# Mixer A of a hybrid decoder: contiguous copies of the normed operands in the dilated order, and attention heads taken two at a time

## The chip, the cores and the metric

The kernel runs on one core of a Trainium2 chip. Five engines work side by side in it: TensorE (PE in the profile; its weight loads are listed as PEld), VectorE (DVE), ScalarE (ACT), GpSimd (POOL) and SyncE (SP), which issues most of the DMAs. The metric is the device time of one execution in microseconds (us), smaller is better. Times are the median of several runs; rows come from one profiled execution.

## The reference, cut to what matters

A trunk of two layers over 512 tokens of width 1024, all in float32. Each layer is half a SwiGLU, a block of three token mixers A, B and C on the same normed `u`, and another half SwiGLU. The change touches mixer A, dilated attention with 3 groups x 6 heads of 64 columns:

```python
DIL_PAIRS = ((128, 1), (512, 4), (2048, 16))     # (window, dilation), 6 heads each
u = rms_norm(h, g_mix)
proj = u @ w_in
a = proj[..., :A_IN].reshape(B, S, 3, A_GROUPS, A_SLOTS, HEAD_DIM)
qa, ka = apply_rope(a[:, :, 0], cos, sin), apply_rope(a[:, :, 1], cos, sin)
o_a = dilated_attention(qa, ka, a[:, :, 2])
...
# dilated_attention: for each group, keys gathered by stride `dil`
    o, lse = banded_attention(to_sub(q), to_sub(k), to_sub(v), BLOCK_Q, n_prev, steps)
alpha = softmax(stack(lses), axis=0)             # the groups of a head are combined
o = sum(alpha[..., None] * stack(outs), axis=0)
```

Group 0 (dilation 1) works on the tokens in their order, groups 1 and 2 on the tokens `c, c+4, c+8, ...` for c = 0 to 3.

## The kernel before, in words

**Products in three parts.** Every large product is made of three float32r matmuls: each operand is split into a high part and the rest, and high x high, low x high and high x low are added up in PSUM. The normed activations lie as eight pairs of tiles `gh[k]`, `gl[k]` (128 features x 512 tokens), the weights are split as they arrive (`whi` on ACT in line 358, `wlo` on DVE in line 359).

**Input projections.** `project_in` multiplies with the activations as the stationary operand: for 8 blocks k of features and 4 blocks j of 128 tokens it issues three matmuls (line 649 ff.), with the 128 tokens of block j as weights of the array and 384 (or 512, 280) columns of `w_in` moving. With `dil` true, block j is every fourth token: the stationary operand is read from `gh` and `gl` with a step of 4 elements. That is so for the groups g = 1 and 2 of mixer A and for nothing else: 3 head pairs p x 2 groups x 8 k x 4 j x 2 layers = 384 such triples of matmuls, all with 384 moving columns.

**Mixer A's attention.** A unit `a_unit(l, p)` does two heads (h = 0 and 1, rows 0 to 63 and 64 to 127 of the tiles `qa`) over all three groups; there are 6 units. All its matmuls are in plain float32, which the trace shows as two records of a weight load and a matmul each. First the scores: for each head, each kind of group (`grp` 1: groups 1 and 2 together; 0: group 0) and each pair `ip` of query blocks, one PSUM bank `sps` is filled by matmuls that contract over the head's 64 rows; DVE adds the mask and takes the minimum (line 1336), ACT makes the exponentials (line 1338) into a tile `ea`. Then four small matmuls with `selT`, a chain of small DVE operations, four with `sel` (`ay`), and on POOL the scaling of the `ea` tiles (line 1370). Last, for each head and block, up to four transposes of `ea` into a bank `tps`, a copy `pa` (DVE or ACT), and up to four matmuls `pv` that write the head's 64 rows of the bank `ops`; the weights there are 64 columns of V, and 128 columns of `pa` move.

**Order of the work.** PE's instructions run in the order in which the program writes them. `weave` merges two things into that order: the stream of projections (`proj`, `project_in`) and the units of attention, which are generators that give up their turn with an estimated delay (`yield "", 1200`); the delay is counted on a clock that `mm` advances with each matmul. The other engines' instructions are ordered by a scheduler. Units wait for flags (`self.done`), so that much of a unit of mixer A for p = 0 or 1 has other projections between its pieces, but its last part has little: the next projection waits for the unit's end.

**Buffers.** PSUM has 4 banks `acc` (projections), 1 `sps`, 2 `tps`, 1 `ops`. The pool of the mixers (`mp`) is opened in `begin_mix`, at the first projection of mixer C.

Of the kernel before, what the change touches and what calls it, by code (L numbers as in the profile page):

```python
# [17 lines left out]
KD = D // 128  # L18
# [37 lines left out]
class Trunk:  # L56
# [567 lines left out]
    def project_in(self, l, cols, kn, dil, evac, pre=None, post=None, ready=None, after=()):  # L624
# [7 lines left out]
        def entries():  # L632
            for ci, k0 in enumerate(range(0, KD, kn)):
                srcs, o = [], 0
                for c, w in cols:
                    srcs.append((o, w, W[k0 * 128:(k0 + kn) * 128, c:c + w]))
                    o += w

                def use(hi, lo, k0=k0, ci=ci):
                    if k0 == 0:  # L640
                        if pre:
                            pre()
                        ps.extend(self.acc() for _ in range(4))
# [159 lines left out]
    def c_inputs(self, l, p):  # L803
# [338 lines left out]
    def b_cmp_probs(self, l, g):  # L1142
        nc = self.nc

        def make(U):
# [18 lines left out]
            small = lambda n: mp.tile([128, 4, 4], F32, tag=n, name=n, bufs=2)  # L1164
# [137 lines left out]
    def a_unit(self, l, p):  # L1302
        nc = self.nc

        def make(U):
# [6 lines left out]
            for h in range(2):  # L1312
                rows = slice(64 * h, 64 * h + 64)
                for grp in (1, 0):
                    for ip in range(2):
                        ps = self.sps()
                        e = mp.tile([128, 512], F32, tag="nq", name="ea", bufs=4) if h else self.et("ea")
                        spans = []
                        for iq in range(2):
                            i = 2 * ip + iq  # L1320
                            c0 = iq * 256 + (128 if grp == 0 and i == 0 else 0)
                            n = iq * 256 + 256 - c0
                            qc = slice(i * 128, (i + 1) * 128)
                            if grp == 0:
                                self.mm(ps[:, c0:c0 + n], qk[0][0][rows, qc],
                                        qk[0][1][rows, (i + 1) * 128 - n:(i + 1) * 128], start=True, stop=True)
                            else:
                                for g in range(2):
                                    self.mm(ps[:, c0 + g * 128:c0 + (g + 1) * 128], qk[1 + g][0][rows, qc],
                                            qk[1 + g][1][rows, qc], start=True, stop=True)  # L1330
                            spans.append((i, slice(c0, c0 + n), n))
# [7 lines left out]
                        es[grp, h, ip] = e  # L1339
                        yield "", 1200  # L1340
# [54 lines left out]
            def pv(h, grp, ip, lo, pa):  # L1395
                rows = slice(64 * h, 64 * h + 64)
                for c in range(lo, 512, 128):
                    iq, b = divmod(c // 128, 2)
                    i = 2 * ip + iq
                    if grp == 0:  # L1400
                        self.mm(Ov[rows, i], vs[0][:, i - 1 + b, rows], pa[:, c:c + 128],
                                start=(ip == 0 and c == lo), stop=False, skip_group_check=True)
                    else:
                        self.mm(O[rows, i * 128:(i + 1) * 128], vs[1 + b][:, i, rows], pa[:, c:c + 128],
                                start=False, stop=(ip == 1 and c == 384), skip_group_check=True)

            for n, (h, grp, ip) in enumerate(todo):
                T = self.tps()
                lo = 128 if grp == 0 and ip == 0 else 0
                for c in range(lo, 512, 128):  # L1410
                    self.transpose(T[:, c:c + 128], es[grp, h, ip][:, c:c + 128])
                pa = mp.tile([128, 512], F32, tag=("ph", "pl")[n % 2], name="pa", bufs=1)
                if n % 2:
                    nc.vector.tensor_copy(pa[:, lo:], T[:, lo:])
                else:
                    nc.scalar.activation(pa[:, lo:], T[:, lo:], AF.Copy)
                if pas:
                    pv(*pas.pop())
                pas.append((h, grp, ip, lo, pa))
                yield "", 1300  # L1420
# [22 lines left out]
    def begin_mix(self, l):  # L1443
# [9 lines left out]
        for u in range(2):  # L1453
# [4 lines left out]
            self.pz.append((ph, pl))  # L1458

# [162 lines left out]
```

## Time and profile before

| what | value |
|---|---|
| time, median of 3 runs (lowest to highest) | 2948.06 us (2946.42 to 2949.58) |
| profiled execution: time | 2947.3 us |
| profiled execution: span of the records | 2945.6 us |
| mean granted TensorE clock, share of full speed | 0.997 |
| PE busy, share of the span | 99% |
| PEld busy | 85% |
| DVE, ACT, POOL busy | 50%, 40%, 17% |
| DMA, mean share of the 16 engines over the span | about 30% |

The profiled execution's own time is 1.7 us above its span and 0.8 us below the median. The busy share of PE counts matmuls that overlap one another, so it says that PE had always something under way, not how fast it went. How fast it goes is read from the distance of the starts of successive matmuls, called the step below.

### The profile page before, as it was taken

How to read it: one execution, taken by the hardware profiler on the slowest of the kernel's cores; microseconds unless marked ns; L12 is line 12 of the kernel's file. 1: busy time of each engine (PE TensorE's matmuls, PEld its weight loads, DVE VectorE, ACT ScalarE, POOL GpSimd, SP SyncE). 2: the span in 40 equal slices, each digit the busy share in tenths (PEclk: the TensorE clock that was granted, in tenths of full speed). 3: DMA queues.
4: the chain of work that ended last, by engine and by line, in shares of the span. 5: the costliest groups of instructions: out<-in, count | busy, mean ns of one | idle time of the engine just before them, and what ended most of it. 6: DMA issues, size and time to landing. Idle time of an engine off the chain costs nothing.

```text
span 2945.6 us, 38966 instructions
## 1 busy us (share of the span) xinstructions
PE 2910.4 (99%) x14281; PEld 2499.2 (85%) x14281; DVE 1459.1 (50%) x2861; ACT 1175.6 (40%) x2405; POOL 506.4 (17%) x657
## 2 busy tenths in 40 slices
PE   8999999999999999999999999999999999999998
PEld 7888898898899888888888888988988998888886
DVE  5464356556633455444354434565665334644433
ACT  4333255455533334333233333554554333333332
POOL 2120012223210322110011100122231112311100
PEclk9999999999999999999999999999999999999999
DMA  4333333321222243333333333332123122433332
GB/s 123 100 94 105 108 97 88 106 63 62 76 60 54 74 126 102 98 97 96 101 93 94 100 103 118 90 101 85 54 65 83 49 56 72 146 97 95 99 93 79
DMA packets 295119, 265.14 MB, mean 90 GB/s; under 512 B 14232, under 2 KB 278544, under 8 KB 294928
## 3 DMA queue, kind: packets, MB, share of 16 engines
q1 hardware_dynamic: 289152, 255.05, 29.7%
q10 hardware_dynamic: 5776, 7.60, 0.7%
q8 instruction: 112, 1.84, 0.3%
q14 instruction: 79, 0.65, 0.1%
HBM read 248.97 MB, written 13.63 MB: 89 GB/s over the span
## 4 chain that ended last, share of the span: by engine, by line
PE 95%; issue 2%; DVE 1%; POOL 1%; ACT 0%; DMA 0%; ACTq 0%; DVEq 0%; POOLq 0%
PE acc L82 66%; PE ops L82 9%; PE tps L82 8%; PE sps L82 8%; PE tps L102 4%; DVE wlo L359 0%; POOL e L853 0%; POOL ss L292 0%; ACT whi L358 0%; DMA gr<-in_cmp_pe_v_dram 0%; POOL e L850 0%; POOL f L850 0%; PE acc L102 0%; DVE x L1084 0%; DVE cf L1087 0%
## 5 line engine op out<-in xcount | busy, mean ns | idle before, releaser
L359 DVE TENSOR_TENSOR wlo<-raw,whi 128x512 fp32r<-128x512 f32 (+3 forms) x944 | 650.7, 694 | 937.1 <-ACT whi L358 887.6
L358 ACT ACTIVATE whi<-raw 128x512 fp32r<-128x512 f32 (+3 forms) x944 | 565.3, 602 | 1113.3 <-PE acc L82 819.6
L82 PE MATMUL acc<-gh,whi 128*128 128x512 f32 x1088 | 430.7, 396 | 0.0
L82 PE MATMUL acc<-gh,wlo 128*128 128x512 f32 x1088 | 424.5, 390 | 0.0
L82 PE MATMUL acc<-gl,whi 128*128 128x512 f32 x1088 | 424.3, 390 | 0.0
L82 PE MATMUL acc<-whi,gh 128*128 128x384 f32 (+2 forms) x960 | 365.7, 381 | 0.0
L82 PE MATMUL acc<-wlo,gh 128*128 128x384 f32 (+2 forms) x960 | 350.1, 365 | 0.0
L82 PE MATMUL acc<-whi,gl 128*128 128x384 f32 (+2 forms) x960 | 350.0, 365 | 0.0
L530 POOL TENSOR_TENSOR a<-a,Rb 128x512 f32<-128x512 f32 x88 | 130.2, 1503 | 907.2 <-DVE a L529 907.2
L82 PE MATMUL acc<-hh,whi 128*128 128x512 f32 x704 | 274.2, 390 | 0.0
L82 PE MATMUL acc<-hh,wlo 128*128 128x512 f32 x704 | 273.9, 389 | 0.0
L82 PE MATMUL acc<-hl,whi 128*128 128x512 f32 x704 | 273.9, 389 | 0.0
L82 PEld LDWEIGHTS acc<-whi,gh 128*128 128x128 f32 x960 | 233.5, 243 | 13.6 <-issue 6.3
L82 PEld LDWEIGHTS acc<-gh,wlo 128*128 128x128 f32 x1088 | 204.2, 188 | 43.8 <-DVE wlo L359 0.2
L82 PEld LDWEIGHTS acc<-wlo,gh 128*128 128x128 f32 x960 | 235.6, 245 | 5.2
L82 PEld LDWEIGHTS acc<-whi,gl 128*128 128x128 f32 x960 | 235.9, 246 | 4.6
L82 PEld LDWEIGHTS acc<-gh,whi 128*128 128x128 f32 x1088 | 204.6, 188 | 39.8 <-issue 1.0
L82 PEld LDWEIGHTS acc<-gl,whi 128*128 128x128 f32 x1088 | 204.6, 188 | 38.2
L82 PEld LDWEIGHTS acc<-hh,wlo 128*128 128x128 f32 x704 | 132.2, 188 | 27.5
L82 PEld LDWEIGHTS acc<-hh,whi 128*128 128x128 f32 x704 | 132.2, 188 | 27.2
L82 PEld LDWEIGHTS acc<-hl,whi 128*128 128x128 f32 x704 | 132.2, 188 | 27.2
L82 PE MATMUL tps<-gh,whi 128*128 128x512 f32 x320 | 124.5, 389 | 0.0
(354 smaller groups left out, 4599.9 us busy)
## 6 DMA issues: line engine op xcount, KB each, us to landing
raw<-in_ffn_w_dram SPq DMA_DIRECT2D x256, 512.0 KB, 3.7
raw<-in_w_in_dram SPq DMA_DIRECT2D x288, 128.0 KB, 2.4
raw<-in_w_gate_dram SPq DMA_DIRECT2D x48, 512.0 KB, 3.5
raw<-in_w_in_dram SPq DMA_DIRECT2D x16, 512.0 KB, 3.7
raw<-in_w_out_dram SPq DMA_DIRECT2D x16, 512.0 KB, 4.2
gate<-gt ACTq DMA_DIRECT2D x28, 256.0 KB, 2.2
gt<-gate SPq DMA_DIRECT2D x28, 256.0 KB, 3.1
raw<-in_w_up_dram SPq DMA_DIRECT2D x16, 384.0 KB, 3.2
```

The source lines that it names most:

```text
L82: self.nc.tensor.matmul(out, lhsT, rhs, start=start, stop=stop, **kw)
L102: self.nc.tensor.transpose(out, in_, self.ident[:n, :n])
L358: nc.scalar.activation(hi, x, AF.Copy)
L359: nc.vector.tensor_tensor(lo, x, hi.bitcast(F32), op=ALU.subtract)
L530: nc.gpsimd.tensor_tensor(v[j], v[j], self.Rb, op=ALU.mult)
```

## The change

Four edits:

1. A new function `dilate` copies the eight tiles `gh[k]` into eight new tiles `gd[k]` on POOL, in the order in which every fourth token stands together. It is called as the projection of mixer C for p = 1 begins. `project_in` takes its high part from `gd` where `dil` is true, as a contiguous block of 128 columns; the low part `gl` is still read with the step of 4.
2. In the scores of `a_unit` the loop over the heads is the innermost one: matmuls of head 0 (bank `sps`) and head 1 (bank `tps`) alternate, and a turn ends after both heads (an estimated delay of 2400 instead of 1200).
3. The last part does the same: transposes of both heads into the two banks `tps`, a copy of head 0 on ACT and of head 1 on DVE, then `pv` with the heads alternating; four turns with a delay of 2600 instead of eight of 1300. Two more tags hold the copies.
4. Room for the `gd` tiles: two small tiles of mixer B get one buffer instead of two, and a scratch area for DMA descriptors is made smaller.

```diff
@@ project_in
                             xh, xl = tok(self.gh[g], j), tok(self.gl[g], j)
+                            if dil:
+                                xh = self.gd[g][:, j * 128:(j + 1) * 128]
                             self.mm(p, xh, hi[k], start=(g == 0), stop=False)
                             self.mm(p, xl, hi[k], start=False, stop=False)
                             self.mm(p, xh, lo[k], start=False, stop=(g == KD - 1))
@@ c_inputs, pre
             if p == 0:
                 self.begin_mix(l)
+            elif p == 1:
+                self.dilate()
@@ a_unit, scores
-            for h in range(2):
-                rows = slice(64 * h, 64 * h + 64)
-                for grp in (1, 0):
-                    for ip in range(2):
-                        ps = self.sps()
...
+            for grp in (1, 0):
+                for ip in range(2):
+                    pss = (self.sps(), self.tps())
...
+                        for g in range(2) if grp else (None,):
+                            for h, ps in enumerate(pss):
+                                rows = slice(64 * h, 64 * h + 64)
+                                if grp == 0:
+                                    self.mm(ps[:, c0:c0 + n], qk[0][0][rows, qc],
+                                            qk[0][1][rows, (i + 1) * 128 - n:(i + 1) * 128], start=True, stop=True)
+                                else:
                                     self.mm(ps[:, c0 + g * 128:c0 + (g + 1) * 128], qk[1 + g][0][rows, qc],
                                             qk[1 + g][1][rows, qc], start=True, stop=True)
...
-                        yield "", 1200
+                    yield "", 2400
@@ a_unit, last part
-            todo = [(h, grp, ip) for h in range(2) for grp in range(2) for ip in range(2)]
+            todo = [(grp, ip) for grp in range(2) for ip in range(2)]
...
+                    for h in range(2):
+                        rows = slice(64 * h, 64 * h + 64)
+                        if grp == 0:
+                            self.mm(Ov[rows, i], vs[0][:, i - 1 + b, rows], pa[h][:, c:c + 128],
+                                    start=(ip == 0 and c == lo), stop=False, skip_group_check=True)
...
+                for h in range(2):
+                    T = self.tps()
+                    for c in range(lo, 512, 128):
+                        self.transpose(T[:, c:c + 128], es[grp, h, ip][:, c:c + 128])
...
+                yield "", 2600
@@ new function
+    def dilate(self):
+        self.gd = []
+        for k in range(KD):
+            t = self.mp.tile([128, 512], F32R, tag=f"gd{k}", name="gd")
+            self.nc.gpsimd.tensor_copy(t.rearrange("p (c m) -> p m c", c=4), self.gh[k].rearrange("p (m c) -> p m c", c=4))
+            self.gd.append(t)
```

On PE, the first scores of the first unit (p = 0 of layer 0), with the end of the dilated projection before them and its continuation behind. Before (`acc<-whi,gh` reads: bank `acc`, from the weights' high part moving and `gh` standing):

```order
L82 MATMUL acc<-whi,gh 128x384
L82 MATMUL acc<-whi,gl 128x384
L82 MATMUL acc<-wlo,gh 128x384
L82 MATMUL sps<-qa 128x128 x4
L82 MATMUL acc<-whi,gh 128x384
L82 MATMUL acc<-whi,gl 128x384
```

and now:

```order
L82 MATMUL acc<-whi,gd 128x384
L82 MATMUL acc<-whi,gl 128x384
L82 MATMUL acc<-wlo,gd 128x384
L82 MATMUL sps<-qa 128x128
L82 MATMUL tps<-qa 128x128
L82 MATMUL sps<-qa 128x128
L82 MATMUL tps<-qa 128x128
L82 MATMUL sps<-qa 128x128
L82 MATMUL tps<-qa 128x128
L82 MATMUL sps<-qa 128x128
L82 MATMUL tps<-qa 128x128
```

Two of the three stationary operands of a triple are `gd`; the block of scores has eight matmuls of two heads in turn where it had four of one head, and a unit has four such blocks instead of eight, with 15, 15, 15 and 21 projection matmuls behind them instead of 9 (seven times) and 15.

On PE, the last part of the same unit. Before:

```order
L102 MATMUL tps<-ident,ea 128x128 x4
L82 MATMUL ops<-pa,va 64x32x4 x3
L102 MATMUL tps<-ident,nata 128x128 x4
L102 MATMUL tps<-ident,ea 128x128 x4
L82 MATMUL ops<-pa,va 64x32x4 x4
L102 MATMUL tps<-ident,ea 128x128 x4
L82 MATMUL ops<-pa,va 64x128 x4
L102 MATMUL tps<-ident,nata 128x128 x4
```

and now:

```order
L102 MATMUL tps<-ident,ea 128x128 x8
L82 MATMUL ops<-pa,va 64x32x4 x6
L82 MATMUL acc<-whi,gd 128x384
L82 MATMUL acc<-whi,gl 128x384
L82 MATMUL acc<-wlo,gd 128x384
L102 MATMUL tps<-ident,nata 128x128 x4
L102 MATMUL tps<-ident,ea 128x128 x8
L82 MATMUL ops<-pa,va 64x32x4 x8
L102 MATMUL tps<-ident,nata 128x128 x4
L102 MATMUL tps<-ident,ea 128x128 x8
```

Transposes (`ident,ea`) and `pv` matmuls (`pa,va`) come in blocks twice as long and half as many. In the units for p = 0 and 1 there are 8 blocks of `pv` before and 4 now, in those for p = 2 there are 7 and 4.

On POOL, where the copies stand now in layer 0 (`a<-a,Rb`: the last multiplications of the first half SwiGLU; `f` and `e`: the first masks and products of mixer C):

```order
L530 TENSOR_TENSOR a<-a,Rb 128x512 x8
L1475 COPY gd<-gh 128x128x4 x8
L854 AFFINE_SELECT f<-f 128x128
L854 AFFINE_SELECT e<-e 128x128
L854 AFFINE_SELECT f<-f 128x128
L857 TENSOR_TENSOR e<-e,f 128x127
```

Before, the masks of mixer C came next to those multiplications; now the eight copies are ahead of them in POOL's queue, in both layers.

## Rows read from the trace of the kernel before

**Rows 1.** The profile's page: busy time, share and instructions of PE and PEld, and the shares of the span along the chain that ended last, by engine.

```profile
PE 2910.4 (99%) x14281; PEld 2499.2 (85%) x14281; DVE 1459.1 (50%) x2861; ACT 1175.6 (40%) x2405; POOL 506.4 (17%) x657
...
PE 95%; issue 2%; DVE 1%; POOL 1%; ACT 0%; DMA 0%; ACTq 0%; DVEq 0%; POOLq 0%
```

**Rows 2.** PE's instructions in order of time (start us, duration us, engine, line, op, out<-in, shapes). First an unbroken run of 30 matmuls of a dilated projection, its first and its last; then an unbroken run of 95 of a projection in token order (group 0), its first and its last.

```profile
816.74 0.40 PE L82 MATMUL acc<-whi,gh 128*128 128x384 f32 x1
...
823.51 0.40 PE L82 MATMUL acc<-wlo,gh 128*128 128x384 f32 x1
...
889.31 0.34 PE L82 MATMUL acc<-whi,gl 128*128 128x384 f32 x1
...
905.60 0.34 PE L82 MATMUL acc<-wlo,gh 128*128 128x384 f32 x1
```

**Rows 3.** Groups of weight loads (count | busy us, mean ns of one): in a stretch of the second run of rows 2, in a stretch of the first, and over the whole program.

```profile
L82 PEld LDWEIGHTS acc<-wlo,gh 128*128 128x128 f32 x31 | 5.8, 188 | 0.0
...
L82 PEld LDWEIGHTS acc<-wlo,gh 128*128 128x128 f32 x9 | 3.0, 330 | 0.0
...
L82 PEld LDWEIGHTS acc<-wlo,gh 128*128 128x128 f32 x960 | 235.6, 245 | 5.2
```

**Rows 4.** The place where a projection in token order ends (816.56 is its last matmul) and a dilated one begins: PE and then PEld in order of time. The load that starts at 816.57 is the first with a step, that of the matmul at 816.74.

```profile
816.56 0.34 PE L82 MATMUL acc<-wlo,gh 128*128 128x384 f32 x1
...
816.97 0.41 PE L82 MATMUL acc<-whi,gl 128*128 128x384 f32 x1
...
816.39 0.19 PEld L82 LDWEIGHTS acc<-wlo,gh 128*128 128x128 f32 x1
816.57 0.31 PEld L82 LDWEIGHTS acc<-whi,gh 128*128 128x128 f32 x1
816.78 0.33 PEld L82 LDWEIGHTS acc<-whi,gl 128*128 128x128 f32 x1
817.02 0.33 PEld L82 LDWEIGHTS acc<-wlo,gh 128*128 128x128 f32 x1
```

**Rows 5.** The chain of waits in the first unit of mixer A, in order of time (start us, length us, engine and bank, line, records): blocks of scores (`sps`, 8 records are 4 matmuls) and the projection between them, and the 21 projection matmuls between the small matmuls with `selT` and those with `sel`.

```profile
837.51 1.09 PE sps L82 x8
838.59 2.36 PE acc L82 x9
840.95 1.08 PE sps L82 x8
...
866.77 5.07 PE acc L82 x21
```

**Rows 6.** Groups over the whole program (records | busy us, mean ns of one): the matmuls of scores and of `pv`, the `selT` matmuls, the weight loads of both, and the copies `pa` out of a bank `tps` on DVE.

```profile
L82 PE MATMUL ops<-pa,va 128*64 128x128 f32 x360 | 49.2, 279 | 0.0
L82 PE MATMUL sps<-qa 64*128 64x128 f32 x216 | 33.5, 289 | 0.7 <-DVE asm L1336 0.7
L82 PE MATMUL sps<-qa 64*128 64x256 f32 x72 | 20.7, 394 | 0.0
...
L82 PE MATMUL tps<-asm,selT 128*128 128x16 f32 x48 | 5.8, 252 | 0.0
...
L82 PEld LDWEIGHTS ops<-pa,va 128*64 128x64 f32 x360 | 38.0, 136 | 7.7 <-issue 7.4 <-ACT whi L358 0.3
L82 PEld LDWEIGHTS sps<-qa 64*128 64x128 f32 x288 | 37.4, 187 | 12.8 <-issue 8.8 <-DVE wlo L359 1.4 <-PE acc L82 1.1
...
L1414 DVE COPY pa<-tps 128x512 f32<-128x512 f32 x24 | 16.5, 689 | 25.9 <-PE tps L102 25.9
```

**Rows 7.** Runs of like records on PE, merged, from the start of the first to the end of the last: inside a block of scores of 128 columns (six records), of scores of 256 columns (three), of the `selT` matmuls with 16 moving columns (seven), and of `pv` (six); then, whole, a block of `pv`, one of transposes and the next of `pv`.

```profile
837.76 0.83 PE L82 MATMUL sps<-qa 64*128 64x128 f32 x6
...
861.40 0.81 PE L82 MATMUL sps<-qa 64*128 64x256 f32 x3
...
865.84 0.93 PE L82 MATMUL tps<-asm,selT 128*128 128x16 f32 x7
...
886.67 0.82 PE L82 MATMUL ops<-pa,va 128*64 128x128 f32 x6
...
886.41 1.09 PE L82 MATMUL ops<-pa,va 128*64 128x128 f32 x8
887.42 0.66 PE L102 MATMUL tps<-ident,nata 128*128 128x128 f32 x4
888.01 1.09 PE L82 MATMUL ops<-pa,va 128*64 128x128 f32 x8
```

**Rows 8.** POOL ahead of mixer C in layer 0 (the bracket is its idle time before the row and what ended it), the last of the tiles `gh` on ACT, and POOL's group of 128x512 products.

```profile
414.59 0.29 POOL L850 TENSOR_SCALAR_AFFINE_SELECT f<-f 128x128 f32<-128x128 f32 x1 [159.10 <-ACT f L849]
...
382.87 0.71 ACT L330 ACTIVATE gh<-h,G 128x512 fp32r<-128x512 f32 x1
...
L530 POOL TENSOR_TENSOR a<-a,Rb 128x512 f32<-128x512 f32 x88 | 130.2, 1503 | 907.2 <-DVE a L529 907.2
```

**Rows 9.** The chain behind the scores of the first unit: the small DVE operation that is last before the `sel` matmuls, POOL's scaling of the `ea` tiles (8 operations for the two heads' group 0, 8 for groups 1 and 2), and the `sel` matmuls on PE.

```profile
870.55 0.18 DVE L1365 TENSOR_TENSOR ay<-ad,cmask 128x32 f32<-128x32 f32 x1
...
870.29 3.45 POOL L1370 TENSOR_SCALAR ea<-ea,ad 128x128 f32<-128x128 f32 x8 [24.06 <-ACT nata L1255]
873.72 4.27 POOL L1370 TENSOR_SCALAR ea<-ea,aw 128x256 f32<-128x256 f32 x8
...
871.68 0.95 PE L82 MATMUL tps<-ay,sel 128*128 128x8 f32 x8
```

More of the change, by code (lines that the diff above doesn't have):

```diff
@@ L1163, in make @@
             shp = [128, 4, 4, 32]
-            small = lambda n: mp.tile([128, 4, 4], F32, tag=n, name=n, bufs=2)
+            small = lambda n: mp.tile([128, 4, 4], F32, tag=n, name=n, bufs=1)
             mx, ls = small("cmx"), small("cls")
@@ L1311, in make @@
             es = {}
-            for h in range(2):
-                rows = slice(64 * h, 64 * h + 64)
-                for grp in (1, 0):
-                    for ip in range(2):
-                        ps = self.sps()
[L1317 to L1328, printed above, removed]
+            for grp in (1, 0):
+                for ip in range(2):
+                    pss = (self.sps(), self.tps())
+                    es[grp, 0, ip] = self.et("ea")
+                    es[grp, 1, ip] = mp.tile([128, 512], F32, tag="nq", name="ea", bufs=4)
+                    spans = []
+                    for iq in range(2):
+                        i = 2 * ip + iq
+                        c0 = iq * 256 + (128 if grp == 0 and i == 0 else 0)
+                        n = iq * 256 + 256 - c0
+                        qc = slice(i * 128, (i + 1) * 128)
+                        for g in range(2) if grp else (None,):
[5 more added lines that the diff above has]
+                                else:
@@ L1329, in make @@
                                     self.mm(ps[:, c0 + g * 128:c0 + (g + 1) * 128], qk[1 + g][0][rows, qc],
                                             qk[1 + g][1][rows, qc], start=True, stop=True)
-                            spans.append((i, slice(c0, c0 + n), n))
+                        spans.append((i, slice(c0, c0 + n), n))
+                    for h, ps in enumerate(pss):
+                        e = es[grp, h, ip]
                         for i, cs, n in spans:
@@ L1338, in make @@
                             nc.scalar.activation(e[:, cs], e[:, cs], AF.Exp, bias=nm, scale=-1.0, accum_out=ls)
-                        es[grp, h, ip] = e
-                        yield "", 1200
+                    yield "", 2400
             yield "", 500
@@ L1391, in make, with pv @@
             Ov = O.rearrange("p (c i r) -> p i r c", c=4, r=32)
-            todo = [(h, grp, ip) for h in range(2) for grp in range(2) for ip in range(2)]
+            todo = [(grp, ip) for grp in range(2) for ip in range(2)]
             pas = []
-            def pv(h, grp, ip, lo, pa):
-                rows = slice(64 * h, 64 * h + 64)
+            def pv(grp, ip, lo, pa):
                 for c in range(lo, 512, 128):
@@ L1399, in pv @@
                     i = 2 * ip + iq
-                    if grp == 0:
-                        self.mm(Ov[rows, i], vs[0][:, i - 1 + b, rows], pa[:, c:c + 128],
-                                start=(ip == 0 and c == lo), stop=False, skip_group_check=True)
-                    else:
[L1404 to L1416, printed above, removed]
+                    for h in range(2):
[3 more added lines that the diff above has]
+                                    start=(ip == 0 and c == lo), stop=False, skip_group_check=True)
+                        else:
+                            self.mm(O[rows, i * 128:(i + 1) * 128], vs[1 + b][:, i, rows], pa[h][:, c:c + 128],
+                                    start=False, stop=(ip == 1 and c == 384), skip_group_check=True)
@@ new lines, in make @@
+            for n, (grp, ip) in enumerate(todo):
+                lo = 128 if grp == 0 and ip == 0 else 0
+                pa = []
+                for h in range(2):
+                    T = self.tps()
+                    for c in range(lo, 512, 128):
+                        self.transpose(T[:, c:c + 128], es[grp, h, ip][:, c:c + 128])
+                    pa.append(mp.tile([128, 512], F32, tag=(("ph", "pl"), ("pch", "pcl"))[n % 2][h], name="pa", bufs=1))
+                    if h:
+                        nc.vector.tensor_copy(pa[h][:, lo:], T[:, lo:])
+                    else:
+                        nc.scalar.activation(pa[h][:, lo:], T[:, lo:], AF.Copy)
@@ L1417, in make @@
                 if pas:
                     pv(*pas.pop())
-                pas.append((h, grp, ip, lo, pa))
-                yield "", 1300
+                pas.append((grp, ip, lo, pa))
+                yield "", 2600
             pv(*pas.pop())
@@ L1609 @@
     from concourse.bass_utils import run_bass_kernel_spmd as _run
-    nc = _bacc.Bacc("TRN2", target_bir_lowering=False, num_devices=1)
+    nc = _bacc.Bacc("TRN2", target_bir_lowering=False, num_devices=1, dynamic_dma_scratch_size=64)
     arrays, ins = {}, {}
```

## The prediction, made before the changed kernel had run

> **What bounds the kernel now.** I read the page first. PE is busy for 99% of the span, and 95% of the chain that ended last is PE itself [rows 1]; the other engines hold half of their time or less. So the time falls only where PE's own instructions come faster, and rises where PE is made to wait. A busy PE hides how fast it goes, so the second reading is the step, the distance between the starts of successive matmuls. In token order 95 matmuls of 384 columns start between 889.31 and 905.60: 16.29 / 94 = 0.173 us a step. In the dilated order 30 of the same shape start between 816.74 and 823.51: 6.77 / 29 = 0.233 [rows 2]. The third view says why: the weight load takes 188 ns in the one stretch and 330 in the other [rows 3]. The mean over all 960 loads of this kind, 245 ns, is what 576 at 188 and 384 at 330 give, so all dilated triples are slow alike. Last, mixer A's small float32 blocks: the chain goes straight from one PE block to the next, so each of them is on the path [rows 5].
>
> **1. The copies, on POOL.** Eight copies a layer, ahead of mixer C's first mask. The trace has none like them. In layer 0 POOL has idled 159.10 us before that mask at 414.59, and the last `gh` is ready at 382.87 + 0.71 = 383.58 [rows 8]: 31.0 us for eight, 3.9 each. POOL's nearest row, a product of the same size, takes 1.50; eight are 12.0 us, hidden. Without that cover up to 12 us a layer would stand before mixer C's chain. I take 0.
>
> **2. Two contiguous loads of three.** At the border of the two orders the trace shows one load with a step behind contiguous ones. It starts at 816.57, just behind the matmul at 816.56, and its own matmul starts at 816.74: a step of 0.18. Only the next, with a second such load, is at 816.97, 0.23 later, since its load could not start before 816.78, 0.21 after the first [rows 4, 2]. So a single slow load fits beside a running matmul; what paces the stream is two in a row. In the new triple the slow one (`gl`) always follows a `gd`. The load behind it is contiguous and can start some 0.04 after the slow one's matmul, and a load with almost nothing to stream behind it paces at 0.11 ((0.93 - 0.25) / 6, the `selT` matmuls) [rows 6, 7], so it is there at 0.15, before the stream needs it at 0.173. A triple then costs 3 x 0.174 = 0.52 instead of 0.70. Upper bound of the gain: 384 x 0.179 = 69 us. Lower bound, if the matmul with the slow load keeps its 0.233: 384 x (0.70 - 0.58) = 46 us. I take 67, near the upper end, because the border row shows just this order.
>
> **3. Fewer blocks.** A block of four scores and nine projection matmuls repeat every 837.51 to 840.95 = 3.44 us [rows 5]. Nine steps of 0.233 are 2.10; eight score records at (0.83 - 0.28) / 5 = 0.11 are 0.89 [rows 6, 7]; the rest, 0.45, is going into the 64-row mode and back. Twenty-four such blocks go (8 to 4 in 6 units); the restart behind a block begins with a contiguous load now, so I take 0.42 each: 10 us. In the last part, `pv` and transposes start at 886.41, 887.42 and 888.01: 1.01 for eight records, which at 0.11 ((0.82 - 0.28) / 5) are 0.87, and 0.59 for four transposes at the same step, 0.44 [rows 7]. So 0.14 and 0.15 are changes of mode, and 4 x 4 + 2 x 3 = 22 pairs of blocks less give 6.5. Together 17; bounds 12 and 21.
>
> **4. Two heads side by side.** Score and `pv` records cost 216 x 0.11 + 72 x 0.21 ((0.81 - 0.39) / 2) + 360 x 0.11 = 23.8 + 15.1 + 39.6 = 78.5 us [rows 6, 7]. Nothing in the trace shows two halves of the array at work together. Bounds: no gain, and half of it, 39 us. Between them stands the load. A load of 128 columns paces at 0.11 however little streams [rows 7]; a load of 64 columns is shorter by 187 - 136 = 51 ns for 64 columns, which is half of that pace [rows 6]. If matmuls overlap but loads go one after another, the scores of 128 columns win nothing, those of 256 go from 0.42 to 0.22 for two records (36 x 0.20 = 7), and `pv` wins its half, 20: 27 us. I take 27: the load is the one thing on these rows that already ties the pace.
>
> By the Trainium skill, TensorE: Matmul & The Clock Gate, section Part 2, step 1, PE pulls a weight load ahead of running matmuls when their row groups don't conflict; scores of the two heads would then run wholly together, and the sum of this part would be the 39 us of the upper bound. The same page's section on LDWEIGHTS says that a load's time goes by its columns and not by its rows, so that half the rows make it no cheaper; here 187 ns for 64 rows stands beside 188 for 128 [rows 6, 3], and by this rule with serial loads the part gives the 27.
>
> **5. What becomes late next.** With PE faster, its cover for the other engines shrinks. Behind the scores, the 21 projection matmuls that take 5.07 us now [rows 5] will take about 3.9; the DVE chain in that gap ends at 870.55 + 0.18, 4.0 after the gap begins, while the `sel` matmuls stood at 871.68 [rows 5, 9]. A few tenths a unit. POOL scales head 0's four operations first: head 1's first two end about 6/8 of 3.45 = 2.6 after the start, and PE now wants them right behind head 0's, so 0 to 1 us a unit. In the last part three users share two `tps` banks: a copy takes 0.69 [rows 6] and four transposes cover 0.44, so some 0.5 twice in the four units for p = 0 and 1. I take +6, bounds 0 and 15. What queues behind PE there are the next projections, nothing else.
>
> **Sum:** -67 - 17 - 27 + 6 = -105. Against the profiled execution's own 2947.3 us (span 2945.6 plus 1.7) this is 2842; the median of the runs is 0.8 above it, so I say 2843.
>
> **Rivals.**
> - *The halves run wholly together.* For it: head 0 and head 1 use separate rows, and separate banks for the scores. Against it: the records of one float32 matmul come in twos on the same half. -67 - 17 - 39 + 6 = -117: 2830. Chance 0.20.
> - *The pairing gives nothing*, the matmuls follow one another as now; the rows of today can't exclude it. -78: 2869. Chance 0.13.
> - *The slow load holds its matmul at 0.233.* Against it: the border row. -46 - 17 - 27 + 6 = -84: 2863. Chance 0.10.
> - *Late chains take part of it back*: 4 us in each unit instead of 1 on DVE and POOL, from which mixer B's last chains, which lie beside the first dilated projections, take some too. -105 + 25: 2867. Chance 0.08.
> - *Slower: each change of heads is a change of mode.* The halves alternate with every matmul, 144 times in the scores and 180 times in `pv`. If each alternation cost what going into a block and out of it does, 0.45 and 0.29, that is 65 + 52 = 117, and with part 4 at nothing the sum is -67 - 17 + 117 + 6 = +39: 2986. It decides from 78 / 324 = 0.24 us an alternation. For it: no block today alternates. Against it: today's price is for a change between 64 and 128 rows or columns, which an alternation is not. Chance 0.04. By the Trainium skill, TensorEngine Tiling (Array Packing), section Key Properties, a change of the tiling mode drains TensorE and a change of tile does not; the blocks' 0.45 agrees with the first half, and no run so far shows the second.
>
> **How the numbers follow.** My forecast, loads in turn and matmuls together, has 0.45; its own range is 2830 to 2856 (the upper end of part 2, both bounds of parts 3 and 5). With the rivals on both sides the range is 2815 (all upper gains, -69 - 21 - 39 + 0 = -129, is 2818) to 2885 (no pairing, and 15 more of lateness); beyond it lie the slower rival and two shortfalls together. About 0.2% is what a measurement of this kernel can tell from no change. All rivals but one are faster by more, so faster 0.95, within it 0.01, slower 0.04.
>
> **What would show it.** Loads of `acc<-whi,gd` at 188 ns and a step of 0.174 through a whole dilated run; if steps go 0.23, 0.17, 0.17, part 2 falls to its lower bound. Blocks of eight score matmuls: 16 records of 128 columns and the mode changes in about 2.2 us if loads take turns, 1.3 if the halves run together, 4 or more if alternation drains. Sixteen `pv` records in 0.9 us. POOL's copies before 400. I am wrong if waits on POOL's `ea` or on `pa` stand before PE's transposes for more than 2 us a unit, or if the step between the two heads is above 0.24.

## Result, and the profile after

| what | before | after |
|---|---|---|
| time, median of 4 runs (lowest to highest) | 2948.06 us (2946.42 to 2949.58) | 2850.78 us (2849.45 to 2852.43) |
| ratio, 95% interval | | 0.967 (0.9654 to 0.9687) |
| span of the profiled execution | 2945.6 us | 2849.2 us |
| granted TensorE clock | 0.997 | 0.996 |

The change saves 97.3 us of the median and 96.4 us of the span. The forecast was 105 less; the range of 2815 to 2885 holds the result.

The page of the changed kernel, busy time and the shares of the chain, as in [rows 1]:

```profile
PE 2810.0 (99%) x14281; PEld 2410.0 (85%) x14281; DVE 1464.4 (51%) x2861; ACT 1170.7 (41%) x2405; POOL 530.8 (19%) x673
...
PE 93%; issue 2%; DVE 2%; POOL 2%; ACT 1%; DMA 1%; DVEq 0%; POOLq 0%; ACTq 0%
```

PE has as many instructions as before and is still busy for 99%: it is the same work at smaller steps. Its share of the chain falls from 95 to 93%, and DVE, POOL, ACT and DMA gain a point each.

**The dilated projections**, in order of time (start us, duration us), first PE, then PEld, as in [rows 2, 4]:

```profile
824.38 0.34 PE L82 MATMUL acc<-whi,gd 128*128 128x384 f32 x1
824.55 0.39 PE L82 MATMUL acc<-whi,gl 128*128 128x384 f32 x1
824.78 0.33 PE L82 MATMUL acc<-wlo,gd 128*128 128x384 f32 x1
824.95 0.34 PE L82 MATMUL acc<-whi,gd 128*128 128x384 f32 x1
```

```profile
824.38 0.31 PEld L82 LDWEIGHTS acc<-whi,gl 128*128 128x128 f32 x1
824.59 0.21 PEld L82 LDWEIGHTS acc<-wlo,gd 128*128 128x128 f32 x1
824.79 0.19 PEld L82 LDWEIGHTS acc<-whi,gd 128*128 128x128 f32 x1
```

A triple takes 824.95 - 824.38 = 0.57 us where it took 0.70. Its steps are 0.17, 0.23, 0.17, not three of 0.174. The loads of the high parts are short (0.19 and 0.21), the one with the step of 4 still takes 0.31, and its own matmul keeps the old step of 0.23 and a duration near the old one (0.39, against 0.34 of its neighbour).

**A block of scores** of both heads, PE in order of time, with the first projection matmul behind it; then the loads of one of its pairs:

```profile
826.77 0.37 PE L82 MATMUL sps<-qa 64*128 64x128 f32 x1
826.77 0.37 PE L82 MATMUL tps<-qa 64*128 64x128 f32 x1
826.98 0.27 PE L82 MATMUL sps<-qa 64*128 64x128 f32 x1
826.99 0.27 PE L82 MATMUL tps<-qa 64*128 64x128 f32 x1
...
827.65 0.27 PE L82 MATMUL sps<-qa 64*128 64x128 f32 x1
...
827.86 0.45 PE L82 MATMUL acc<-whi,gd 128*128 128x384 f32 x1
```

```profile
826.87 0.19 PEld L82 LDWEIGHTS sps<-qa 64*128 64x128 f32 x1
826.88 0.19 PEld L82 LDWEIGHTS tps<-qa 64*128 64x128 f32 x1
```

Head 0 (`sps`) and head 1 (`tps`) start 0.01 apart, the matmuls as well as their loads, and a pair follows the other at (827.65 - 826.98) / 6 = 0.11: what one record cost before [rows 7]. Eight matmuls of two heads take 826.77 to 827.86 = 1.09 us, as long as four of one head took [rows 5].

**The groups** over the whole program (records | busy us, mean ns | idle time before them and what ended it): `pv`, as in [rows 6], and the transposes of `ea`, first of the changed kernel, then of the kernel before:

```profile
L102 PE MATMUL tps<-ident,ea 128*128 128x128 f32 x180 | 27.7, 278 | 4.8 <-DVE qa L1292 1.8 <-POOL ea L1377 1.2 <-ACT qa L1294 1.1
L82 PE MATMUL ops<-pa,va 128*64 128x128 f32 x360 | 25.0, 279 | 0.0
```

```profile
L102 PE MATMUL tps<-ident,ea 128*128 128x128 f32 x180 | 28.5, 278 | 0.6 <-DVE pa L1414 0.6
```

Busy time counts overlapping matmuls once, so half of `pv`'s 49.2 us says that its two halves run together throughout. Ahead of the transposes PE now waits 4.8 us in all instead of 0.6. Where, the chain of waits in the last part of the first unit shows (start us, length us):

```profile
857.99 0.50 ACT qa L1294
...
858.63 0.63 PE tps L102 x4
859.25 1.02 PE ops L82 x16
...
860.90 0.70 DVE qa L1292
...
861.74 0.63 PE tps L102 x4
```

Twice the chain leaves PE for a copy `qa`, 0.50 on ACT and 0.70 on DVE, that frees a bank `tps` for the next transposes. The first of these copies stands on ACT behind a `whi` (0.52) and a `nata` (0.36), which are the pieces of the same chain just ahead of it: it is late by ACT's order as well as by the shared bank.

**POOL**, the copies (start us, length us of the eight):

```profile
381.06 10.19 POOL L1475 CAST gd<-gh 128x512 fp32r<-128x512 f32 x8 [125.69 <-PE acc L82]
413.54 0.29 POOL L854 TENSOR_SCALAR_AFFINE_SELECT f<-f 128x128 f32<-128x128 f32 x1 [22.29 <-ACT f L853]
```

They end at 391.25, 22.29 us before POOL's next instruction.

### The profile page after: what moved, and what is told of

It is laid out like the page before. It is cut to its first block, busy times and chain, and to the rows that moved or that the text cites. A ratio compares the mean times of both kernels' runs of the same rounds, so it can differ in the third digit from the quotient of the medians.

```text
span 2849.2 us, 38972 instructions
## 1 busy us (share of the span) xinstructions
PE 2810.0 (99%) x14281; PEld 2410.0 (85%) x14281; DVE 1464.4 (51%) x2861; ACT 1170.7 (41%) x2405; POOL 530.8 (19%) x673
## 4 chain that ended last, share of the span: by engine, by line
PE 93%; issue 2%; DVE 2%; POOL 2%; ACT 1%; DMA 1%; DVEq 0%; POOLq 0%; ACTq 0%
PE acc L82 65%; PE tps L82 9%; PE ops L82 8%; PE sps L82 7%; PE tps L102 4%; DVE wlo L359 0%; POOL ea L1377 0%; DMA gt<-gate 0%; POOL e L857 0%; ACT whi L358 0%; POOL ec L1175 0%; POOL ss L292 0%; POOL e L854 0%; PE acc L102 0%; DMA x<-in_x_dram 0%
## 5 line engine op out<-in xcount | busy, mean ns | idle before, releaser
L82 PEld LDWEIGHTS acc<-whi,gl 128*128 128x128 f32 x960 | 227.0, 236 | 5.3
L82 PE MATMUL acc<-whi,gh 128*128 128x384 f32 (+2 forms) x576 | 201.7, 350 | 0.0
L82 PE MATMUL acc<-wlo,gh 128*128 128x384 f32 (+2 forms) x576 | 197.4, 343 | 0.6 <-DVE wlo L359 0.6
L82 PE MATMUL acc<-whi,gd 128*128 128x384 f32 x384 | 135.7, 353 | 0.0
L82 PE MATMUL acc<-wlo,gd 128*128 128x384 f32 x384 | 128.4, 334 | 0.0
```

What stands on the lines that cost most here:

```text
L82: self.nc.tensor.matmul(out, lhsT, rhs, start=start, stop=stop, **kw)
```

## Experiments

The theory at the start: each slow load holds its own matmul, so that the copies are worth 49 us, and the two halves of the array run wholly together, so that the pairing is worth the rest.

**The copies alone.** Scores and last part as before, line by line; the function `dilate`, its call, the room made for its tiles and this edit stay:

```diff
+                            if dil:
+                                xh = self.gd[g][:, j * 128:(j + 1) * 128]
```

> The kernel before with the copies alone: gd is made and read, mixer A's unit is as before. Theory X (the slow load keeps its own matmul at about 0.23 us, the lower bound of part 2): a triple takes 0.573 instead of 0.700 us, 384 x 0.127 = 49 us less, 2899. Theory Y (the prediction: a single slow load is hidden, and what the changed kernel lost against it was lost in waits of the units): a triple takes 0.52 and the time is 67 us less, 2881.

Measured: 2896.74 us (2896.14 to 2899.24), ratio 0.9828 (0.9811 to 0.9844), 51.4 less than before.

**The pairs alone.** The changed kernel without the two lines above and without `dilate`.

> The changed kernel without the copies: the two heads side by side, the dilated projections as before. Theory X (halves wholly together, loads too): pairing 39 and fewer blocks 17, less some 4 of lateness: 52 us less, 2896; a pair of score records of 128 columns every 0.11 us. Theory Y (matmuls together, loads in turn): 27 and 17 less 4 = 40 us less, 2908; a pair every 0.22 us in the scores of 128 columns.

Measured: 2899.07 us (2896.99 to 2901.48), ratio 0.9835 (0.982 to 0.9849), 49.1 less than before (2948.14 beside both). The two parts add up to 100.5 against 97.3 for both together: they hardly touch each other, and each is near what the theory gave it, not near the 67 and 40 that the prediction's terms gave.

**Blocks of both heads, but one head after the other.** The same blocks and banks, the heads' loop outside that over the matmuls, in the scores and in `pv`:

```diff
-                        for g in range(2) if grp else (None,):
-                            for h, ps in enumerate(pss):
-                                rows = slice(64 * h, 64 * h + 64)
...
+                    for h, ps in enumerate(pss):
+                        rows = slice(64 * h, 64 * h + 64)
+                        for iq in range(2):
...
```

> The changed kernel with one edit: inside a block all matmuls of head 0 come first, then all of head 1, so that only the seam can overlap. Blocks, banks, copies and projections are those of the changed kernel. If the gain of the pairing is the alternation (39 us by the steps of the rows, 27 by the forecast), the time rises by that: 2890 or 2878. If the gain came from fewer and longer blocks alone, it stays within 5 us of 2851.

Measured: 2865.04 us (2863.3 to 2869.52), ratio 0.9721 (0.9707 to 0.9736): 14 more than the changed kernel, less than either price for the alternation. The first block of scores of this kernel on PE, in order of time; the program lists four matmuls (eight records) into `sps` and then four into `tps`:

```profile
825.37 0.82 PE L82 MATMUL sps<-qa 64*128 64x128 f32 x5
825.92 0.37 PE L82 MATMUL tps<-qa 64*128 64x128 f32 x1
826.03 0.27 PE L82 MATMUL sps<-qa 64*128 64x128 f32 x1
826.13 0.27 PE L82 MATMUL tps<-qa 64*128 64x128 f32 x1
...
826.36 0.72 PE L82 MATMUL tps<-qa 64*128 64x128 f32 x5
827.00 0.44 PE L82 MATMUL acc<-whi,gd 128*128 128x384 f32 x1
```

Head 1's first record starts at 825.92, when three of head 0's records are still to start: it passes them. Three or four records of each head thus lie beside one another, and the block takes 827.00 - 825.37 = 1.63 us, between 1.09 and twice that. So the expectation was missed because it took the order of the program for the order of the work. The same goes for the sentence under "Order of the work" that PE's instructions run in the order in which the program writes them: for matmuls on different halves of the array it holds only roughly.

**Two matmuls of a head in a row.** The alternation made coarser by a factor of two, in the scores and in the same way in `pv`:

```diff
-                        for g in range(2) if grp else (None,):
-                            for h, ps in enumerate(pss):
-                                rows = slice(64 * h, 64 * h + 64)
+                        for h, ps in enumerate(pss):
+                            rows = slice(64 * h, 64 * h + 64)
+                            for g in range(2) if grp else (None,):
...
```

> The changed kernel, with two matmuls (four records) of head 0 and then two of head 1 where it alternates with every matmul; the 256-column scores go with one bank's two blocks at a time. With four matmuls of a head in a row the time had come out at 2865, and head 1's first records stood beside head 0's last three. Theory W (PE runs matmuls of the free half ahead, up to about three records past those that still wait for the busy half): with two matmuls in a row one record at the start of a block is alone and all others run beside one of the other head: 2851 to 2854. Rival V (only the seam between two heads overlaps, whatever the length of the rows of equal heads; a block then keeps most of what four in a row cost): 2858 to 2865.

Measured: 2853.24 us (2849.42 to 2855.5), beside 2850.5 (2849.17 to 2853.07) for the changed kernel run once more:

> The changed kernel itself once more, as the measure for the three kernels beside it, whose steps are of a few us. Both theories: 2851, within 2 us.

PE in the first block of scores of the coarser kernel, where the program lists four records into `sps` ahead of the first into `tps`:

```profile
826.68 0.37 PE L82 MATMUL sps<-qa 64*128 64x128 f32 x1
826.70 0.37 PE L82 MATMUL tps<-qa 64*128 64x128 f32 x1
...
827.88 0.44 PE L82 MATMUL acc<-whi,gd 128*128 128x384 f32 x1
```

Again the first record of head 1 runs ahead of the three of head 0 that come before it in the program. Theory W holds: the block takes 827.88 - 826.68 = 1.20 us instead of 1.09, one record's step of 0.11 more, and the kernel comes out 2.7 us slower with overlapping ranges, so that single matmuls are hardly better than twos. That three is the limit rests on these two kernels alone.

**The low parts contiguous too.** Both operands are read as blocks of 128 columns; the low part is then that of other tokens, so the reordering of the low part is what this kernel leaves out:

```diff
+                                xl = self.gl[g][:, j * 128:(j + 1) * 128]
```

> The changed kernel, with the low part of the dilated operand read as a contiguous block in token order, which leaves the reordering of that low part out of the computation: no weight load has a step any more. Theory X (each load with a step costs its own matmul 0.05 to 0.06 us wherever it stands): triples go from 0.573 to 0.52, 384 x 0.053 = 20 us less, 2831. Theory Y (a single slow load is hidden already): no change, 2851.

Measured: 2830.62 us (2829.58 to 2833.23), ratio 0.9603 (0.9589 to 0.9618), 20 less than the changed kernel, as expected. That is the price of the one slow load that the change leaves in each triple: 20.2 / 384 = 0.053.

**The low part copied instead of the high one.** `dilate` then reads `gl`, and in `project_in`:

```diff
-                                xh = self.gd[g][:, j * 128:(j + 1) * 128]
+                                xl = self.gd[g][:, j * 128:(j + 1) * 128]
```

> The changed kernel with the tiles gd copied from the low parts gl, so that of a triple the first and the third load are slow and stand next to each other across the seam of two triples. The claim of the prediction (what paces is the second of two slow loads in a row): one such pair a triple, as dear as now: 2851. Rival (every slow load costs its own 0.055): 384 x 0.055 = 21 more: 2872.

Measured: 2876.24 us (2873.3 to 2877.69), ratio 0.9756 (0.9742 to 0.9771): 25 more. PE of this kernel:

```profile
824.24 0.34 PE L82 MATMUL acc<-whi,gd 128*128 128x384 f32 x1
824.41 0.40 PE L82 MATMUL acc<-wlo,gh 128*128 128x384 f32 x1
824.64 0.40 PE L82 MATMUL acc<-whi,gh 128*128 128x384 f32 x1
824.88 0.34 PE L82 MATMUL acc<-whi,gd 128*128 128x384 f32 x1
```

Of two slow loads in a row both matmuls take 0.23 to 0.24, the first like the second. A triple takes 824.88 - 824.24 = 0.64, and 384 x (0.64 - 0.573) = 26, close to the 25 lost. The claim of the prediction, that only the second pays, is refuted.

**What a slow load costs: fewer columns.** The dilated triples with 256 moving columns, but for the first matmul of each sum, which keeps 384. In this kernel and the next two the clock that `weave` goes by is advanced as for 384 columns, and the missing columns of the products are what they leave out:

```diff
...
-                            self.mm(p, xl, hi[k], start=False, stop=False)
-                            self.mm(p, xh, lo[k], start=False, stop=(g == KD - 1))
...
+                            cs = slice(0, 256 if dil else n)
+                            self.mm(p[:, cs], xl, hi[k][:, cs], start=False, stop=False)
+                            self.mm(p[:, cs], xh, lo[k][:, cs], start=False, stop=(g == KD - 1))
...
```

> The changed kernel with 256 instead of 384 moving columns in the dilated triples, but for the first matmul of a sum (the last third of the projected columns then lacks most of its products; only the times count). It tells what the slow load of a triple costs. 280 moving columns in token order have a step of 0.128 in the trace of the changed kernel, so 256 should have 0.117. Theory P (the loads pace: after a slow load the next matmul comes 0.23 behind, whatever streams): steps of 0.117, 0.117 and 0.23, 0.464 a triple instead of 0.573; 384 x 0.109 = 42, less 3 for the 48 full matmuls: 2812. Theory Q (the matmul with the slow load takes 0.055 more than its columns need): 0.117, 0.117 and 0.172, 0.406 a triple; 384 x 0.167 = 64 less 3: 2790.

Measured: 2825.55 us (2823.44 to 2827.39), ratio 0.9584 (0.9568 to 0.96). PE of this kernel:

```profile
825.14 0.28 PE L82 MATMUL acc<-whi,gd 128*128 128x256 f32 x1
825.26 0.40 PE L82 MATMUL acc<-whi,gl 128*128 128x256 f32 x1
825.49 0.28 PE L82 MATMUL acc<-wlo,gd 128*128 128x256 f32 x1
825.61 0.34 PE L82 MATMUL acc<-whi,gd 128*128 128x384 f32 x1
825.78 0.34 PE L82 MATMUL acc<-whi,gl 128*128 128x256 f32 x1
825.96 0.28 PE L82 MATMUL acc<-wlo,gd 128*128 128x256 f32 x1
```

The contiguous steps fall to 825.26 - 825.14 = 0.12, the one with the slow load stays at 0.23 (825.26 to 825.49), which is theory P in the steps. The time falls by 25 and not by the 39 that P gave. A good part of the 14 between them is waits, since the projections that cover the units' chains got shorter. PE's waits in this kernel (us in total, times, longest):

```profile
PE tps L82 <- DVE ay L1378: 4.9, 4, 1.6
...
PE sps L82 <- DVE sm L1209: 3.8, 4, 1.3
PE tps L102 <- POOL e L1213: 2.6, 2, 1.3
```

The first and the last of these had not been there, and the second was 2.6, which makes 8.7 us; the rest I have not traced one by one. But the last rows on PE above don't fit P: the slow matmul behind the one full matmul of a sum (825.61, 384 columns) has a step of 825.96 - 825.78 = 0.18. So a third theory, S: the load begins with the matmul ahead of it, takes some 0.24 in any case, and its own columns stream only then. Two mirrored kernels tell P and S apart.

**Only the matmul with the slow load narrow**, and **only the one ahead of it**:

```diff
+                            cs = slice(0, 256 if dil else n)
-                            self.mm(p, xl, hi[k], start=False, stop=False)
+                            self.mm(p[:, cs], xl, hi[k][:, cs], start=False, stop=False)
...
```

> The changed kernel with 256 instead of 384 moving columns in the one matmul of a dilated triple whose weight load is slow (the last third of the projected columns then lacks the low part; only the times count). Theory P (the next matmul comes 0.232 behind the one with the slow load, whatever streams): nothing changes, 2851. Theory S (a slow load begins with the matmul ahead of it and takes 0.242, and only then do its own columns stream; 256 columns are 0.107, 384 are 0.160; so only the matmul ahead covers it): 0.242 - 0.172 + 0.107 = 0.177 for it, a triple of 0.52 instead of 0.573: 384 x 0.055 = 21 less, 2830.

```diff
...
+                            if dil and g:
+                                self.mm(p[:, 0:256], xh, hi[k][:, 0:256], start=False, stop=False)
...
+                            else:
+                                self.mm(p, xh, hi[k], start=(g == 0), stop=False)
```

> The mirror of the kernel beside it: 256 moving columns in the matmul just ahead of the one with the slow load (but for the first of a sum), and 384 in the other two; the last third of the columns then lacks most of high x high, and only the times count. Theory P: 0.117 + 0.232 + 0.170 = 0.519 a triple instead of 0.573; 336 x 0.054 = 18 less, 2833. Theory S: the cover shrinks to 0.117, the matmul with the slow load takes 0.242 - 0.117 + 0.160 = 0.285, a triple 0.572: no change, 2851.

Measured: 2836.71 us (2834.61 to 2837.68), ratio 0.9624 (0.9608 to 0.964), for the first; 2854.21 us (2852.06 to 2856.02), ratio 0.9682 (0.9668 to 0.9696), for the second. PE of the first, then of the second:

```profile
823.82 0.34 PE L82 MATMUL acc<-whi,gd 128*128 128x384 f32 x1
823.99 0.33 PE L82 MATMUL acc<-whi,gl 128*128 128x256 f32 x1
824.16 0.33 PE L82 MATMUL acc<-wlo,gd 128*128 128x384 f32 x1
```

```profile
824.50 0.28 PE L82 MATMUL acc<-whi,gd 128*128 128x256 f32 x1
824.61 0.45 PE L82 MATMUL acc<-whi,gl 128*128 128x384 f32 x1
824.90 0.34 PE L82 MATMUL acc<-wlo,gd 128*128 128x384 f32 x1
```

With less to stream behind a full matmul the slow step is 0.17, and the slow load is paid for; with a short matmul ahead it is 0.29, and narrowing the neighbour won nothing. S holds in the steps (it gave 0.177 and 0.285) and P falls. The first time is 7 us above what S gives, and at least 4.5 of that are waits on PE: 2.1 on POOL's `e` of line 1209 that had not been there, 2.2 instead of 1.2 on POOL's `ea`, 1.8 instead of 0.9 on DVE's `gt`, 3.1 instead of 2.6 on DVE's `sm`.

S has a gap, though. For a slow load behind another slow load, whose matmul has a step of 0.233, it gives 0.242 - 0.233 + 0.160 = 0.17, and the kernel with the low part copied shows 0.24 there (824.64 to 824.88), as the kernel before has 0.233 throughout. What fits every kernel here within 0.01 is a plainer sum: a slow load adds 0.23 to its step, less what a matmul with as many columns as the one ahead takes among contiguous loads, 0.17 for 384 and 0.12 for 256. That makes 0.06 behind 384 columns, whether the load of these was slow or not, and 0.11 behind 256. Why a slow load ahead gives no more cover, no run here shows.

**The order on POOL, and a third bank.** First, both heads of a block scaled one after the other, in both places:

```diff
-            for h in range(2):
-                for ip in range(2):
+            for ip in range(2):
+                for h in range(2):
```

> The changed kernel with POOL scaling the ea tiles block by block, both heads of a block one after the other, instead of head by head. Theory L (POOL's order makes PE wait before the transposes of head 1; the waits that the trace puts down to POOL's ea are 1.2 us in all, and some of the 6 us that the steps of these transposes grew by are of this kind): 1 to 2 us less than the changed kernel, 2849 to 2850, and no wait on POOL's ea left. Rival M (what PE waits for there is the two banks alone, so the wait only gets another name): no difference, 2851.

Measured: 2848.27 us (2845.29 to 2849.4), ratio 0.9663 (0.965 to 0.9676). That is 2 less than the 2850.5 of the changed kernel beside it; the two ranges touch, so the gain is likely and not certain. Then in addition:

```diff
-                    T = self.tps()
+                    T = self.tps() if h else self.sps()
```

> The kernel of the POOL order block by block, and beside it the transposes of head 0 in the last part of a unit go into the bank of the scores, which nobody uses then, so that the two transpose banks are left to head 1 and to the other users. Theory L (the lateness behind the faster blocks is a matter of three users of two banks; waits of 1.8 + 1.1 us for the copies qa, and some 6 us in the steps of these transposes): 4 to 6 us less than the changed kernel, 2845 to 2847. Rival M (the copies behind the transposes, 0.69 us each, are what is late, and another bank only moves the wait to the pv matmuls): 2849 to 2851.

Measured: 2844.2 us (2843.44 to 2845.19), ratio 0.9651 (0.9638 to 0.9664), 6.3 less than the changed kernel and below each of its runs. The transposes of this kernel, in groups, and its chain at the place shown above:

```profile
L102 PE MATMUL tps<-ident,ea 128*128 128x128 f32 x90 | 14.2, 274 | 0.1
L102 PE MATMUL sps<-ident,ea 128*128 128x128 f32 x90 | 13.9, 275 | 0.0
```

```profile
857.00 0.44 PE tps L102 x4
857.44 0.44 PE sps L102 x4
...
858.31 1.02 PE ops L82 x16
```

The 4.8 us of waiting are 0.1, and the chain stays on PE: theory L. Of the kernels that do the whole of the work it is the fastest.

## Why the prediction came out

The total is 8 us off, in a range of 70, but two of its terms were wrong by more than that, in opposite directions. So the sum is close by luck in its two largest terms, while the other three are near what was measured.

**1. Copies on POOL: right.** They took 10.19 us where 12.0 was estimated, ended before 400, and cost nothing.

**2. Two contiguous loads of three: too much, 49 instead of 67.** A triple went from 0.700 to 0.573, and 384 x 0.127 = 49; the copies alone gave 51. The step that failed is the reading of the border row. I took the 0.18 between the matmuls at 816.56 and 816.74 [rows 4] as the price of the slow load of the latter. But the step behind a matmul's start is its own price: the one that paid for the slow load is the next, 816.74 to 816.97 = 0.23, and I gave that to the second slow load. The duration in the row at 816.74, 0.40 against 0.34 [rows 2, 4], said so. The lower bound, with the 0.233 kept, held, and so did the sign that I named for it (steps of 0.23, 0.17, 0.17 in turn), so the rival that I gave 0.10 is the one that came.

**3. Fewer blocks: the right size.** The pairs alone gave 49.1. Of these 39 are the pairing by its steps (below), which leaves 10 for the blocks less the lateness. The lateness of that kernel can be read from its trace: from the start of each of the 180 records of transposes of `ea` to the start of PE's next matmul it is 29.0 us in all, and 21.6 in the kernel with the third bank, where hardly a wait is left. So the blocks are worth about 10 + 7 = 17. It is a remainder, and no run has it by itself.

**4. Two heads side by side: too little, 39 instead of 27.** A pair now costs what one record did: 12 us for the scores of 128 columns, 7.5 for those of 256 and 20 for `pv`, the upper bound. What failed is the assumption that loads take turns. The pace of 0.11 that I read from [rows 7] is a limit of each half, not of the array: the loads of the two heads start 0.01 apart. The rival to which I gave 0.20 is the one that came here. The Trainium skill's rule, TensorE: Matmul & The Clock Gate, Part 2, step 1, that a load is pulled ahead when the row groups don't conflict, would have given the 39. Its statement in the same place that matmuls stay in program order is not what the kernel with one head after the other shows, where a matmul of the free half starts before three of the other half that the program has ahead of it; the measurement decides. And an alternation of heads costs nothing that the rows show, so the slower rival falls. This agrees with the Trainium skill, TensorEngine Tiling (Array Packing), section Key Properties, by which a change of tile alone does not drain TensorE.

**5. Lateness: 6 was said, some 8 came.** The span fell by 96.4, and 49 + 17 + 39 less that leaves 8.6. The steps behind the transposes of `ea`, added up as in 3, are 29.7 us against the 21.6 with the third bank, 8.1 more, and 4.2 of it is seen as waits ahead of them (4.8 against 0.6). The place was right, the two banks with three users, and the third bank and POOL's order give 6.3 back. The waits put down to POOL's `ea` are 1.2 us in all, 0.2 a unit, at the low end of the 0 to 1 that I allowed. The tenths behind the scores did not come: the 21 projection matmuls in that gap take 4.1 and not the 3.9 that I took, and PE has no wait on `ay`; in the kernel with 256 columns it has one, of 4.9 us in all.

So the sum, -67 - 17 - 27 + 6 = -105, should have been -49 - 17 - 39 + 8 = -97. That the forecast was close is owed to errors of 18 and 12 with opposite signs; either alone would still have been within the range (2861 or 2831). The rivals for the two terms, each of which I had priced by itself, would have given -46 - 17 - 39 + 6 = -96 together, 1 us from the result, but I gave no chance to both at once.

## What to carry to other kernels

Price a slow weight load by the pace of such loads in a row (0.23 us here) less the step that the one matmul ahead of it would have among contiguous loads (0.17): 0.06, as measured. Only that matmul covers it, and the price shows in the step behind its own matmul, not in the one before. Slack further back was not saved up: with 256 columns ahead the slow load cost 0.11 and 0.12, although the matmul before those had 256 columns in the one kernel and 384 in the other. When two matmuls use different halves of the array, count their records and loads as running at the same time, and put them within a few records of each other; the exact order matters little. When PE gets faster, look for the small banks that several users share, and give one of them to whoever comes late.

## What the runs showed that I had not expected

- **A load with a step of 4 hides behind one matmul only.** From the start of such a load to the matmul after its own it is 824.78 - 824.38 = 0.40 with 384 columns in the changed kernel. 128 columns fewer take 0.17 - 0.12 = 0.05 off a contiguous step (0.173 to 0.118 over all of them), so 384 take some 0.16 of that 0.40, and the load about 0.24. With that figure the three steps of 0.23, 0.17 and 0.29 (384 behind 384, 256 behind 384, 384 behind 256) follow within 0.01. For a slow load behind another slow one that figure does not do (above).
- **The two halves overlap even where the program doesn't ask for it.** With one head after the other the block of scores still took 1.63 us, not twice 1.09, and the whole kernel lost 14 us, not the 27 or 39 that were put on the pairing.
- **Loads into column halves run together too.** `pv` uses 64 columns for each head. Its matmuls' busy time fell from 49.2 to 25.0 us and that of its loads from 38.0 to 19.2, with 136 ns for one load before and after [rows 6].
